# Conv-side output projection in a new block order, its neighbours' stores on other queues, norm weights spread by DMA

## The chip, the cores and the metric

One Trainium2 chip, one core, one execution of one program. The metric is device microseconds (us) from start to end of an execution. An execution is timed as a whole; the profile of one execution gives its span (first to last instruction) and every instruction in it. Engines in rows: PE is TensorE (PEld its weight loads), DVE is VectorE, ACT is ScalarE, POOL is GpSimd, SP is the engine that here does nothing but issue DMAs (SPq in rows).

## The reference, cut to what matters

```python
h = rms_norm(x, norm1_g)                       # x: 1024 tokens x 1024
u = h @ w_in                                   # conv gate 2x512, then q, k, v, g of 512 each
a_out = conv_group(u_conv, ...)                # GLU, 31 causal taps, layer norm, silu -> 512 wide
b_out = retention_group(q, k, v, g, ...)       # 4 heads, chunks of 64 -> 512 wide
x = x + concat([a_out, b_out]) @ w_out         # output projection
h = rms_norm(x, norm2_g)
x = x + square(relu(h @ w_ff1)) @ w_ff2        # 1024 -> 4096 -> 1024
return rms_norm(x, final_g)
```

All of it is float32.

## The kernel before, in words

A float32 matmul is made of three passes over operands that are split into a high and a low part of a reduced type (`mm3`, L138 to L140: high by high, high by low, low by high). ACT makes the high part by a copy, DVE the low part by a subtraction (`split_evac`, L189 and L190). A matmul that depends on a fresh operand therefore waits for DMA, ACT and DVE in that order; the third pass, or the second, is the one that waits for DVE.

The 1024 tokens are 8 blocks of 128 (`blk[0..7]`). The stages around the change, in time:

1. Input projections, convolution taps and retention. Here ACT, DVE and SP load and split the weights.
2. Output projection, retention half (`ret_side`, L515 to L579), block by block, weights `wo`.
3. The second norm's weights, a vector of 1024, are spread over all partitions as `n2row`: POOL makes eight 128x128 diagonals, PE multiplies each by ones, ACT copies the two banks (L605 to L611).
4. Output projection, conv half, the loop L669 to L681. In iteration b: layer norm of the conv output of block b+3 (`conv_norm`: PE transposes `py`, DVE statistics, POOL reciprocal root, ACT `yn`); its silu and split for block b+2 (`conv_side`: PE transposes `pt`, ACT `a` and `mh`, DVE `ml`); 24 matmuls of 128x512 for block b (`out_proj`); DVE adds them to `blk[b]` (L675); ACT takes the mean square (`trash`), POOL the root (`rn`); then `normed_columns(b - 1)`.
5. `normed_columns(b)` scales the block (DVE `xn`, L624), transposes it on PE (`pt`, L634), and makes columns for FF1, which runs one step of Strassen's scheme: seven products M1 to M7 of half-size operands. Blocks 0 to 3 are tokens of the first half: their columns are the operands B11 and B21 themselves (used by M1 and M2), are split, and are also stored whole to DRAM (`keep_columns`, DMA `colsB<-full`). Blocks 4 to 7 are of the second half. Block 4+t loads the columns of block t back (`b<-colsB`), and DVE forms from both T1, T2, B22, T3 and T4 (seven DVE instructions of 128x512, nine for block 7; called the T work below). T1, T2 and B22 are split in place. T3 and T4 of blocks 4 to 6 go to DRAM (`colsT<-b`), because their tiles come free only later, and return in one load of 768 KB each (`h<-colsT`, L829), after which ACT and DVE split them.
6. FF1, 16 pairs p of weight columns (`strassen_pair`). The first four pairs (AHEAD = 4) do M1 and M2 first, all four of them, since only B11 and B21 are needed; then pair 0 goes on with M6, M5, M7, M3, M4, and so do pairs 1 to 3. The other twelve do all seven products at once. A product is 12 matmuls of 128x512. Each pair's results, 7 tiles, are stored to DRAM (`x0M`, `x1M`, ...).
7. FF2 and the final norm.

Every DMA of the kernel before is issued by SP, in program order of its list: an SP instruction that waits for its data holds all behind it. Within each other engine too, instructions run in one order that a scheduler fixed when the kernel was built, by priorities that follow the order of the code. PSUM is two pools of four banks; `py`, `pt`, the `pb` of M2 and of odd products take one, `acc` and `pa` the other. So a transpose waits until a bank's former content has been read by ACT and DVE.

Of the kernel before, what the change touches and what calls it, by code (L numbers as in the profile page):

```python
# [8 lines left out]
F32 = mybir.dt.float32  # L9
F32R = mybir.dt.float32r  # L10
BF16 = mybir.dt.bfloat16
AF = mybir.ActivationFunctionType
ALU = mybir.AluOpType
PSUM = bass.MemoryType.PSUM

P = 128
D = 1024
# [8 lines left out]
ND = D // P  # L26
NB = S // P
NC = CW // P
NF = FF // P
HALF = 512  # L30
# [3 lines left out]
ALIGN = 256  # L34
QUOTA = (4, 16, 11, 11, 13, 33, 22, 14)
NPAIR = NF // 2
AHEAD = 4


@with_exitstack  # L40
def hybrid_layer_kernel(
# [14 lines left out]
    nc = tc.nc  # L56
# [6 lines left out]
    sp = pool("sp", 11)  # L63
    tiny = pool("tiny", 8)
# [4 lines left out]
    pr = pool("pr", 4, space=PSUM)  # L69
# [80 lines left out]
    def mean_sq(src):  # L150

        tr = sp.tile([P, D], BF16, tag="s", name="trash")
        ss = tiny.tile([P, 1], F32, tag="ss1", name="ss")
        nc.scalar.activation(tr, src, AF.Square, scale=D**-0.5, accum_out=ss)
        return ss
# [86 lines left out]
    def stats(t):  # L242

        nonlocal r1_pair
        xt = cp.tile([P, D], F32, tag="c", name="xt")
        nc.sync.dma_start(xt, x[t * P : (t + 1) * P, :])
        if t % 2 == 0 or t >= 4:
            r1_pair = const.tile([P, 2], F32, name=f"r1_{t}")
            r1[t] = r1_pair[:, 0:1]
        else:  # L250
            r1[t] = r1_pair[:, 1:2]
        m = tiny.tile([P, 1], F32, tag="nmr", name="m1")
        nc.gpsimd.tensor_tensor(m, mean_sq(xt), eps1, ALU.add)
        nc.gpsimd.tensor_tensor(r1[t], m, mhalf[:, 0:1], ALU.pow)
# [67 lines left out]
    nc.sync.dma_start(dec, decay)  # L322
    for t in range(NB):
        stats(t)

    first, accs = accs, [[bank(1)], [bank(1)]]
    for d in range(ND):
# [163 lines left out]
    def out_proj(wo, mh, ml):  # L491
        accs = []
        for n in range(2):
            acc = ps.tile([P, HALF], F32, tag="mm", name="acc")
            for c in range(NC):
                mm3(
                    acc, mh[:, c], ml[:, c],
                    wo[c][:, 0, 0, n * HALF : (n + 1) * HALF],
                    wo[c][:, 1, 0, n * HALF : (n + 1) * HALF],
                    c == 0, c == NC - 1,  # L500
                )
            accs.append(acc)
        return accs
# [34 lines left out]
    def conv_norm(b):  # L538

        py = pr.tile([P, NC, P], F32, tag="r", name="py")  # L540
        for c in range(NC):
            nc.tensor.transpose(out=py[:, c], in_=ys[c][:, b * P : (b + 1) * P], identity=ident)
        st = tiny.tile([P, 6], F32, tag="st", name="st")
        nc.vector.bn_stats(st, py.rearrange("p c e -> p (c e)"))
        mv = tiny.tile([P, 2], F32, tag="mv", name="mv")
        nc.vector.bn_aggr(mv, st)
        r = rstd_of(mv[:, 1:2], 1.0)
        yn = sp.tile([P, CW], F32, tag="s", name="yn")
        nmr = tiny.tile([P, 1], F32, tag="nmr", name="nmr")
        nc.gpsimd.tensor_scalar(nmr, mv[:, 0:1], r[:, 0:1], -1.0, ALU.mult, ALU.mult)  # L550
        nc.scalar.activation(
            yn, py.rearrange("p c e -> p (c e)"), AF.Identity, bias=nmr[:, 0:1], scale=r[:, 0:1]
        )
        normed[b] = yn

    def conv_side(b):

        yn = normed.pop(b)
        pt = pr.tile([P, NC, P], F32, tag="r", name="pt")
        for c in range(NC):  # L560
            nc.tensor.transpose(out=pt[:, c], in_=yn[:, c * P : (c + 1) * P], identity=ident)
        a = sp.tile([P, NC, P], F32, tag="s", name="a")
        for c in range(NC):
            nc.scalar.activation(a[:, c], pt[:, c], AF.Silu, bias=col("lb", c), scale=col("lg", c))
        sides[b] = split_tiles(a)

    marks.append(len(pe_log))
    for b in range(NB):
        if b + 2 < NB:
            rsides[b + 2] = ret_side(b + 2)  # L570
        if b == NB - 2:
            woa = load_wo(0, False)
        if b >= NB - 3:
            conv_norm(b - (NB - 3))
        if b >= NB - 2:
            conv_side(b - (NB - 2))
        (mh, ml), xr = rsides.pop(b)
        for n, acc in enumerate(out_proj(wo, mh, ml)):
            nc.vector.tensor_tensor(blk[b][:, n], acc, xr[n], ALU.add)  # L579
# [22 lines left out]
    dram_cols = {nm: xd.tile([P, 4, HALF], F32, name=f"cols{nm}") for nm in ("B11", "B21", "T3", "T4")}  # L602

    n2row = cp.tile([P, D], F32, tag="c", name="n2row")
    for g in range(2):  # L605
        pb = pr.tile([P, 4, P], F32, tag="r", name="pb")
        for i in range(4):
            diag = sp.tile([P, P], F32, tag="s", name="diag")
            nc.gpsimd.tensor_scalar(diag, ident, col("n2", 4 * g + i), None, ALU.mult)
            nc.tensor.matmul(pb[:, i], lhsT=ones, rhs=diag, start=True, stop=True)  # L610
        nc.scalar.activation(n2row[:, g * HALF : (g + 1) * HALF], pb.rearrange("p i t -> p (i t)"), AF.Copy)  # L611

    def new_columns(name, extra=False):
        hb[name] = [wp.tile([P, 4, HALF], F32R, tag="w", name="h2") for _ in range(1 if extra else 2)]
# [1 line left out]
            hb[name].append(hx.tile([P, 4, HALF], F32R, name="tx"))  # L616

    def keep_columns(name, cols, t):
        nc.sync.dma_start(dram_cols[name][:, :, cols], t)

    def normed_columns(b, r):

# [39 lines left out]
        for name, full in (("T3", b12), ("T4", b21)):  # L662
            if b < NB - 1:
                keep_columns(name, cols, full)
            else:
                split_evac(full, *hl(name))

    rn = {}
    for b in range(NB):  # L669
        if b + 3 < NB:  # L670
            conv_norm(b + 3)
        if b + 2 < NB:
            conv_side(b + 2)
        for n, acc in enumerate(out_proj(woa, *sides.pop(b))):
            nc.vector.tensor_tensor(blk[b][:, n], acc, blk[b][:, n], ALU.add)  # L675
        m = tiny.tile([P, 1], F32, tag="nmr", name="m2")
        nc.gpsimd.tensor_tensor(m, mean_sq(flat(b)), eps1, ALU.add)
        rn[b] = tiny.tile([P, 1], F32, tag="r1", name="rn")
        nc.gpsimd.tensor_tensor(rn[b], m, mhalf[:, 0:1], ALU.pow)
        if b >= 1:  # L680
            normed_columns(b - 1, rn.pop(b - 1))  # L681

# [29 lines left out]
    def split_named(ops, raw, names):  # L714
        hi, lo = split_pairs(raw)
        for k, nm in enumerate(names):
            ops[nm] = hi[:, k], lo[:, k]
# [12 lines left out]
    xs = {}  # L730

    def keep(p, name, t):
        nc.sync.dma_start(xs[p][name], t)

    def square(src, rl=None):

# [27 lines left out]
    def strassen_pair(p, ahead):  # L764

        a, b = {}, hb

        def product(acc, name, first, last):
            for d in range(4):
                mm3(  # L770
                    acc, a[name][0][:, d], a[name][1][:, d], b[name][0][:, d], b[name][1][:, d],
                    first and d == 0, last and d == 3, loose=True,
                )

        def copy(acc):
            t = sp.tile([P, HALF], F32, tag="s", name="part")
            nc.scalar.activation(t, acc, AF.Copy)
            return t

        def plus(acc, t):  # L780
            nc.vector.tensor_tensor(t, acc, t, ALU.add)
            return t

        raw = [load_w1(2 * p + i) for i in range(1 if ahead else 2)]
        split_named(a, raw[0], ("M1", "M2"))
        if not ahead:
            prep_sums(a, raw)
        pa = ps.tile([P, HALF], F32, tag="mm", name="pa")
        product(pa, "M1", True, False)
        m1 = copy(pa)  # L790
        pb = pr.tile([P, HALF], F32, tag="r", name="pb")
        product(pb, "M2", True, True)
        c11 = square(plus(pb, m1))
        if p < NPAIR - 1:
            keep(p, "M1", c11)
        if ahead:
            yield
            prep_sums(a, [load_w1(2 * p + i) for i in range(2)])
            c11 = sp.tile([P, HALF], F32, tag="s", name="hid")
            nc.sync.dma_start(c11, xs[p]["M1"])  # L800
        product(pa, "M6", False, False)
        u2 = copy(pa)
        pb = pr.tile([P, HALF], F32, tag="r", name="pb")
        product(pb, "M5", True, False)
        m5 = copy(pb)
        product(pa, "M7", False, False)
        c22 = square(plus(pa, m5))
        product(pb, "M3", False, True)
        c12 = square(plus(pb, u2))
        product(pa, "M4", False, True)  # L810
        c21 = square(pa, relu(pa))
        if p < NPAIR - 1:
            keep_operands(p, c11, c12, c21, c22)
        else:
            for i, row in enumerate(((c11, c12), (c21, c22))):
                for j, t in enumerate(row):
                    nc.sync.dma_start(last_hid[i][:, j * HALF : (j + 1) * HALF], t)

    last_hid = [xd.tile([P, S], F32, name=f"hid{i}") for i in range(2)]
    for p in range(NPAIR):  # L820
        new_operands(p)
    pairs = [strassen_pair(p, p < AHEAD) for p in range(NPAIR)]
    hb["M1"], hb["M2"] = hb["B11"], hb["B21"]
    next(pairs[0])
    for name in ("T3", "T4"):
# [2 lines left out]
    for name in ("T3", "T4"):  # L828
        nc.sync.dma_start(hb[name][1][:, :, early].bitcast(F32), dram_cols[name][:, :, early])  # L829
    normed_columns(NB - 1, rn.pop(NB - 1))  # L830
    for p in range(1, AHEAD):
        next(pairs[p])
    for name in ("T3", "T4"):
        hi, lo = (t[:, :, early] for t in hb[name])
# [201 lines left out]
```

## Time and profile before

| | us |
|---|---|
| median of 3 runs | 1069.08 (1068.64 to 1069.27) |
| profiled execution, its own time | 1070.16 |
| its span in the trace | 1068.4 |
| PE busy | 1036.5 (97%) |
| DVE busy | 805.9 (75%) |
| ACT busy | 378.9 (35%) |
| POOL busy | 69.7 (7%) |
| mean granted clock of PE | 0.987 |

Times in the rows count from the start of the span. The profiled execution lies 1.08 us above the median. PE is busy almost throughout; where it isn't, or where its granted clock falls, is what the rows below show, stage by stage.

### The profile page before, as it was taken

The numbers are of one execution on the slowest core, as the hardware profiler recorded it, in microseconds if no ns is written. First come the engines' busy times: TensorE is split into PE (matmuls) and PEld (weight loads), VectorE is DVE, ScalarE is ACT, GpSimd is POOL, SyncE is SP. The second block draws the span as 40 slices with busy tenths as digits, with TensorE's granted clock in tenths as the row PEclk, the third lists the DMA queues.
The fourth block names the chain that finished last, engine by engine and source line by source line (L and its number), as shares of the span: only waits on it lengthen the run. The fifth ranks groups of instructions, "written<-read, shape, count | busy, mean of one in ns | idle before, by whom it ended". The sixth has DMA issues, their size and how long they took to land.

```text
span 1068.4 us, 12644 instructions
## 1 busy us (share of the span) xinstructions
PE 1036.5 (97%) x4760; PEld 858.1 (80%) x4760; DVE 805.9 (75%) x998; ACT 378.9 (35%) x602; POOL 69.7 (7%) x134
## 2 busy tenths in 40 slices
PE   9999999999999997899999999999999999999996
PEld 7888888888888775677888888888788888888885
DVE  6397769998796367866777676776898778777857
ACT  7511111144521565432332333323443333433423
POOL 0400110022000311000000000000000000000003
PEclk9999999999999999889999999999999999999998
DMA  9412011002242013635545344356546355253324
GB/s 359 162 45 79 20 59 60 21 1 80 65 152 79 1 60 114 195 136 178 195 143 183 138 161 145 137 178 232 182 164 246 104 177 176 92 183 102 91 78 157
DMA packets 59676, 136.98 MB, mean 128 GB/s; under 512 B 5600, under 2 KB 18016, under 8 KB 59616
## 3 DMA queue, kind: packets, MB, share of 16 engines
q1 hardware_dynamic: 59616, 136.19, 37.0%
q8 instruction: 37, 0.61, 0.2%
q14 instruction: 23, 0.19, 0.1%
HBM read 99.73 MB, written 36.44 MB: 127 GB/s over the span
## 4 chain that ended last, share of the span: by engine, by line
PE 50%; DVE 3%; DMA 3%; issue 2%; ACT 1%; POOL 1%; SPq 0%; POOLq 0%; DVEq 0%; ACTq 0%
PE acc L138 9%; PE acc L140 9%; PE acc L139 9%; PE pa L140 5%; PE pa L139 5%; PE pa L138 5%; PE pb L140 3%; PE pb L139 3%; PE pb L138 3%; DMA raw<-in_w_dram 2%; DMA xr<-x1M 1%; DVE w1l L190 1%; DVE ot L933 0%; DVE hid L740 0%; DMA w2raw<-in_w_dram 0%
## 5 line engine op out<-in xcount | busy, mean ns | idle before, releaser
L138 PE MATMUL acc<-w 128*128 128x512 f32 x454 | 176.7, 389 | 1.1 <-ACT w L189 1.1
L139 PE MATMUL acc<-w 128*128 128x512 f32 x454 | 176.2, 388 | 0.0
L140 PE MATMUL acc<-w 128*128 128x512 f32 x454 | 175.9, 388 | 0.0
L380 DVE SCALAR_TENSOR_TENSOR y<-glu,vec,y 128x1024 f32<-128x1024 f32 x120 | 153.8, 1290 | 2.0
L138 PEld LDWEIGHTS acc<-w 128*128 128x128 f32 x454 | 85.2, 188 | 20.1 <-ACT w L189 1.5
L138 PE MATMUL acc<-w,cols 128*128 128x512 f32 x256 | 100.1, 391 | 0.0
L139 PE MATMUL acc<-w,cols 128*128 128x512 f32 x256 | 99.8, 390 | 0.0
L140 PE MATMUL acc<-w,cols 128*128 128x512 f32 x256 | 99.7, 390 | 0.0
L139 PEld LDWEIGHTS acc<-w 128*128 128x128 f32 x454 | 85.2, 188 | 17.5
L140 PEld LDWEIGHTS acc<-w 128*128 128x128 f32 x454 | 85.2, 188 | 17.5
L189 ACT ACTIVATE w<-xr 128x1024 fp32r<-128x1024 f32 (+1 forms) x56 | 56.2, 1004 | 107.4 <-PE acc L140 57.9
L140 PE MATMUL pa<-h,w1l 128*128 128x512 f32 x192 | 77.8, 405 | 11.6 <-DVE w1l L190 11.6
L190 DVE TENSOR_TENSOR w<-xr,w 128x1024 fp32r<-128x1024 f32 (+1 forms) x56 | 64.7, 1155 | 28.1 <-ACT w L189 27.9
L905 DVE TENSOR_TENSOR blk<-acc,blk 128x512 f32<-128x512 f32 x112 | 72.8, 686 | 11.7 <-PE acc L140 11.7
L138 PE MATMUL pa<-h,w1h 128*128 128x512 f32 x192 | 77.0, 402 | 0.1
L140 PE MATMUL pb<-h,w1l 128*128 128x512 f32 x192 | 75.5, 393 | 0.0
L138 PE MATMUL pb<-h,w1h 128*128 128x512 f32 x192 | 75.3, 392 | 0.0
L139 PE MATMUL pb<-h,w1h 128*128 128x512 f32 x192 | 75.2, 392 | 0.0
L115 ACT ACTIVATE w<-raw 128x1024 fp32r<-128x1024 f32 (+1 forms) x36 | 34.8, 967 | 96.2 <-PE acc L140 70.5
L189 ACT ACTIVATE w1h<-t 128x1024 fp32r<-128x1024 f32 x32 | 33.8, 1059 | 65.9 <-PE pb L140 40.5
L140 PEld LDWEIGHTS acc<-w,cols 128*128 128x128 f32 x256 | 48.1, 188 | 10.0
L138 PEld LDWEIGHTS acc<-w,cols 128*128 128x128 f32 x256 | 48.1, 188 | 9.8
(175 smaller groups left out, 1962.7 us busy)
## 6 DMA issues: line engine op xcount, KB each, us to landing
raw<-in_w_dram SPq DMA_DIRECT2D x38, 512.0 KB, 3.5
w2raw<-in_w_dram SPq DMA_DIRECT2D x30, 512.0 KB, 4.5
raw<-in_w_in_dram SPq DMA_DIRECT2D x23, 512.0 KB, 3.3
xt<-in_x_dram SPq DMA_DIRECT2D x8, 512.0 KB, 7.7
raw<-in_w_out_dram SPq DMA_DIRECT2D x8, 512.0 KB, 3.3
xr<-in_x_dram SPq DMA_DIRECT2D x16, 256.0 KB, 3.1
out_dram<-ot SPq DMA_DIRECT2D x16, 256.0 KB, 2.0
xcol<-in_x_cols_dram SPq DMA_DIRECT2D x7, 512.0 KB, 7.2
```

Of the source, the lines that this page charges most:

```text
L115: nc.scalar.activation(w[:, 0, i], raw[:, i], AF.Copy)
L138: nc.tensor.matmul(acc, lhsT=lh, rhs=rh, start=first, stop=False, **kw)
L139: nc.tensor.matmul(acc, lhsT=lh, rhs=rl, start=False, stop=False, **kw)
L140: pe_log.append(nc.tensor.matmul(acc, lhsT=ll, rhs=rh, start=False, stop=last, **kw))
L189: nc.scalar.activation(hi, src, AF.Copy)
L190: nc.vector.tensor_tensor(lo, src, hi.bitcast(F32), ALU.subtract)
L380: nc.vector.scalar_tensor_tensor(y, glu[c][:, k : k + S], tap(k), y, ALU.mult, ALU.add)
L905: nc.vector.tensor_tensor(t, acc[lane][r], t, ALU.add)
```

## The change

Four edits. (1) The loop of stage 4 visits the blocks in the order 0 1 4 2 5 3 6 7, and so do the layer norms and silus ahead of it. The loop's code now stands behind the creation of the pairs. (2) `colsB` is stored from ACT's queue, `colsT`, all results of FF1 and the last hidden tiles from POOL's; SP keeps the loads. (3) `n2row` is made without PE: eight columns of the small-vector tile are written to DRAM as 1024 numbers near the start, on SP behind the token loads, and read back spread over all partitions. (4) The first W1 tiles of pairs 0 and 1 are loaded and split inside the loop, at its last two iterations, and those of pairs 2 and 3 one step sooner than their products.

```diff
+ORDER = (0, 1, 4, 2, 5, 3, 6, 7)
...
     for t in range(NB):
         stats(t)
+    n2d = xd.tile([D], F32, name="n2d")
+    nc.sync.dma_start(n2d.rearrange("(d p) -> p d", p=P), vec[:, cols["n2"] : cols["n2"] + ND])
...
     n2row = cp.tile([P, D], F32, tag="c", name="n2row")
-    for g in range(2):
-        pb = pr.tile([P, 4, P], F32, tag="r", name="pb")
-        for i in range(4):
-            diag = sp.tile([P, P], F32, tag="s", name="diag")
-            nc.gpsimd.tensor_scalar(diag, ident, col("n2", 4 * g + i), None, ALU.mult)
-            nc.tensor.matmul(pb[:, i], lhsT=ones, rhs=diag, start=True, stop=True)
-        nc.scalar.activation(n2row[:, g * HALF : (g + 1) * HALF], pb.rearrange("p i t -> p (i t)"), AF.Copy)
+    nc.sync.dma_start(n2row, n2d.partition_broadcast(P))
...
     def keep_columns(name, cols, t):
-        nc.sync.dma_start(dram_cols[name][:, :, cols], t)
+        eng = nc.scalar if name in ("B11", "B21") else nc.gpsimd
+        eng.dma_start(dram_cols[name][:, :, cols], t)
...
     def keep(p, name, t):
-        nc.sync.dma_start(xs[p][name], t)
+        nc.gpsimd.dma_start(xs[p][name], t)
...
         split_named(a, raw[0], ("M1", "M2"))
+        if ahead:
+            yield
...
     pairs = [strassen_pair(p, p < AHEAD) for p in range(NPAIR)]
+    rn = {}
+    for i, b in enumerate(ORDER):
+        if i + 3 < NB:
+            conv_norm(ORDER[i + 3])
+        if i + 2 < NB:
+            conv_side(ORDER[i + 2])
...
+        if i >= 6:
+            next(pairs[i - 6])
+        if i >= 1:
+            normed_columns(ORDER[i - 1], rn.pop(ORDER[i - 1]))
```

What this does to the engines' orders, at three places. (Line numbers differ by one to twenty between the two kernels; the number behind a name tells tiles apart.)

DVE, where the T work of block 4 stands. Before, it begins behind block 5's `xn_3377` and goes on among the sums of block 6, the seventh in order (`pt_3312` are block 4's columns; `h2_2981` belongs to block 3):

```order
L190 TENSOR_TENSOR h2_2981<-pt_3241,h2_2980 128x4x128
L675 TENSOR_TENSOR blk5_106<-acc_3270,blk5_106 128x512
L190 TENSOR_TENSOR ml_3267<-a_3261,mh_3266 128x512
L675 TENSOR_TENSOR blk5_106<-acc_3283,blk5_106 128x512
L624 SCALAR_TENSOR_TENSOR xn_3377<-blk5_106,rn_3303,n2row_2805 128x1024
L655 TENSOR_TENSOR b11_3323<-b12_3327,b11_3323 128x512
L675 TENSOR_TENSOR blk6_107<-acc_3342,blk6_107 128x512
L656 TENSOR_TENSOR t2_3328<-pt_3312,b11_3323 128x512
L659 TENSOR_TENSOR b12_3327<-pt_3312,b12_3327 128x512
```

DVE now: the same T work (`pt_3186` are block 4's columns) stands between block 2's `xn_3282` and block 2's own columns (`pt_3284`, `pt_3289`).

```order
L622 SCALAR_TENSOR_TENSOR xn_3282<-blk2_103,rn_3177,n2row_2807 128x1024
L653 TENSOR_TENSOR b11_3197<-b12_3201,b11_3197 128x512
L815 TENSOR_TENSOR blk5_106<-acc_3247,blk5_106 128x512
L654 TENSOR_TENSOR t2_3202<-pt_3186,b11_3197 128x512
L657 TENSOR_TENSOR b12_3201<-pt_3186,b12_3201 128x512
L658 TENSOR_TENSOR b21_3198<-b21_3198,t2_3202 128x512
L191 TENSOR_TENSOR tx_3192<-t2_3202,h2_3191 128x4x128
L191 TENSOR_TENSOR h2_3194<-b11_3197,h2_3193 128x4x128
L815 TENSOR_TENSOR blk5_106<-acc_3260,blk5_106 128x512
L191 TENSOR_TENSOR h2_3196<-pt_3186,h2_3195 128x4x128
L191 TENSOR_TENSOR h2_3012<-pt_3284,h2_3011 128x4x128
```

It moved from among the seventh block's sums to among the fifth's (block 5), two blocks up, and stands ahead of the splits that free the banks of block 2's transposes.

DVE at the first M1. Before, its low weights `w1l_3535` stand behind the T work of blocks 4 and 5 and among that of block 6 (`b11_3455`):

```order
L190 TENSOR_TENSOR h2_3322<-pt_3384,h2_3321 128x4x128
L655 TENSOR_TENSOR b11_3455<-b12_3459,b11_3455 128x512
L190 TENSOR_TENSOR w1l_3535<-raw_3532,w1h_3534 128x1024
L656 TENSOR_TENSOR t2_3460<-pt_3450,b11_3455 128x512
L190 TENSOR_TENSOR h2_3320<-b11_3455,h2_3319 128x4x128
```

Now `w1l_3422` (pair 0) stands ahead of the last two blocks' sums, and `w1l_3485` (pair 1) ahead of the T work of blocks 6 and 7:

```order
L815 TENSOR_TENSOR blk3_104<-acc_3331,blk3_104 128x512
L191 TENSOR_TENSOR w1l_3422<-raw_3419,w1h_3421 128x1024
L191 TENSOR_TENSOR ml_3315<-a_3309,mh_3314 128x512
L815 TENSOR_TENSOR blk6_107<-acc_3384,blk6_107 128x512
...
L815 TENSOR_TENSOR blk7_108<-acc_3460,blk7_108 128x512
L191 TENSOR_TENSOR w1l_3485<-raw_3482,w1h_3484 128x1024
L622 SCALAR_TENSOR_TENSOR xn_3488<-blk6_107,rn_3417,n2row_2807 128x1024
L622 SCALAR_TENSOR_TENSOR xn_3557<-blk7_108,rn_3480,n2row_2807 128x1024
L653 TENSOR_TENSOR b11_3500<-b12_3504,b11_3500 128x512
```

PE's order there, before (the last of the projection, `acc_3421`, then block 6's transposes, then M1 of pair 0 in `pa_3538` begun with two matmuls, M2 in `pb_3553` with two):

```order
L140 MATMUL acc_3421<-w_2676,ml_3267 128x512
L634 MATMUL pt_3445<-ident_89,xn_3443 128x128 x4
L634 MATMUL pt_3450<-ident_89,xn_3443 128x128 x4
L138 MATMUL pa_3538<-h2_2978,w1h_3534 128x512
L139 MATMUL pa_3538<-h2_2979,w1h_3534 128x512
L138 MATMUL pb_3553<-h2_2980,w1h_3534 128x512
L139 MATMUL pb_3553<-h2_2981,w1h_3534 128x512
L140 MATMUL pa_3538<-h2_2978,w1l_3535 128x512
```

and now: M1 of pair 0 (12 matmuls in `pa_3519`) follows the projection at once, then half of pair 1's M1 (`pa_3590`), and only then block 6's transposes.

```order
L141 MATMUL acc_3460<-w_2678,ml_3315 128x512
L139 MATMUL pa_3519<-h2_3011,w1h_3421 128x512
...
L141 MATMUL pa_3590<-h2_3011,w1l_3485 128x512
L632 MATMUL pt_3490<-ident_89,xn_3488 128x128 x4
L632 MATMUL pt_3495<-ident_89,xn_3488 128x128 x4
L139 MATMUL pb_3534<-h2_3013,w1h_3421 128x512
```

SP's queue before, from block 6's store of T3 on:

```order
L619 DMA colsT3_2803<-b12_3459 512x1x128
L619 DMA colsT4_2804<-b21_3456 512x1x128
L829 DMA h2_3571<-colsT3_2803 128x4x384
L829 DMA h2_3573<-colsT4_2804 128x4x384
L733 DMA x0M1_3476<-hid_3567 128x512
L651 DMA b11_3588<-colsB11_2801 128x4x128
```

and now, loads only:

```order
L687 DMA raw_3660<-in_w1_dram 128x1024
L830 DMA h2_3552<-colsT3_2805 128x4x384
L830 DMA h2_3554<-colsT4_2806 128x4x384
L649 DMA b11_3569<-colsB11_2803 128x4x128
```

The return of T3 and T4 (`h2_3552`, `h2_3554`) still waits for block 6's stores, which POOL now issues.

## Rows read from the trace of the kernel before

**Rows 1.** Windows of 20 us: their length; PE, PEld, DVE, ACT, POOL busy; PEclk; DMA.
```profile
400.00:420.00 20.00, 17.78 (x86) 14.27 (x84) 12.35 (x18) 11.17 (x23) 2.18 (x6) 1.00 0.37 107
420.00:440.00 20.00, 14.82 (x59) 11.79 (x60) 17.69 (x23) 10.17 (x15) 0.77 (x3) 0.74 0.63 204
440.00:460.00 20.00, 15.76 (x58) 12.15 (x56) 14.57 (x22) 8.25 (x12) 0.00 (x0) 0.83 0.38 123
```

**Rows 2.** PE's waits over the whole run: us in total, times, longest.
```profile
PE pa L140 <- DVE w1l L190: 11.6, 5, 3.8
PE pt L634 <- DVE xn L624: 3.7, 2, 2.3
```

**Rows 3.** Timeline of PE between the halves: start, duration, instruction, [idle before].
```profile
357.47 0.61 PE L610 MATMUL pb<-diag,ones 128*128 128x128 f32 x4
...
361.65 0.60 PE L542 MATMUL py<-ident,y 128*128 128x128 f32 x4
...
362.44 0.48 PE L138 MATMUL acc<-w,mh 128*128 128x512 f32 x1
...
363.22 0.39 PE L138 MATMUL acc<-w,mh 128*128 128x512 f32 x1
363.44 0.39 PE L139 MATMUL acc<-w,mh 128*128 128x512 f32 x1
```

**Rows 4.** Timeline of PE, from block 4's columns to M6.
```profile
412.70 1.06 PE L634 MATMUL pt<-ident,xn 128*128 128x128 f32 x8 [1.46 <-DVE xn L624]
...
418.85 0.39 PE L140 MATMUL acc<-w,ml 128*128 128x512 f32 x1
421.50 1.15 PE L634 MATMUL pt<-ident,xn 128*128 128x128 f32 x8 [2.27 <-DVE xn L624]
...
428.04 0.79 PE L140 MATMUL pa<-h,w1l 128*128 128x512 f32 x1 [3.67 <-DVE w1l L190]
...
432.05 0.63 PE L140 MATMUL pa<-h,w1l 128*128 128x512 f32 x1
432.47 0.46 PE L140 MATMUL pb<-h,w1l 128*128 128x512 f32 x1
...
461.81 0.50 PE L140 MATMUL pa<-h,w1l 128*128 128x512 f32 x1 [2.27 <-DVE w1l L190]
```

**Rows 5.** Timeline of DVE: T work of block 4, then pieces towards M6.
```profile
412.48 0.69 DVE L655 TENSOR_TENSOR b<-b,b 128x512 f32<-128x512 f32 x1
413.08 0.68 DVE L675 TENSOR_TENSOR blk<-acc,blk 128x512 f32<-128x512 f32 x1
...
416.68 0.68 DVE L190 TENSOR_TENSOR h<-pt,h 128x512 fp32r<-128x512 f32 x1
...
432.70 1.22 DVE L190 TENSOR_TENSOR w1l<-raw,w1h 128x1024 fp32r<-128x1024 f32 x1
...
451.91 1.75 DVE L190 TENSOR_TENSOR h<-h,h 128x1536 fp32r<-128x1536 f32 x1
```

**Rows 6.** Timeline of ACT: the split of T3 waits for its load; block 6's copy.
```profile
424.23 0.58 ACT L654 ACTIVATE b<-pt 128x512 f32<-128x512 f32 x1
...
437.16 1.49 ACT L189 ACTIVATE h<-h 128x1536 fp32r<-128x1536 f32 x1 [2.90 <-DMA h<-colsT]
```

**Rows 7.** Timeline of SP's queue: block 6's stores, the loads.
```profile
429.82 1.71 SPq L619 DMA_DIRECT2D colsT<-b  x2
432.52 1.62 SPq L829 DMA_DIRECT2D h<-colsT  x2
```

**Rows 8.** DMA issues: KB each, median us from issue to landing.
```profile
x3M<-xsum SPq DMA_DIRECT2D x8, 256.0 KB, 3.0
...
colsT<-b SPq DMA_DIRECT2D x6, 256.0 KB, 2.5
h<-colsT SPq DMA_DIRECT2D x2, 768.0 KB, 5.4
```

**Rows 9.** A window near the start, columns as rows 1.
```profile
34.00:38.00 4.00, 4.00 (x20) 3.30 (x19) 0.00 (x0) 0.00 (x0) 3.50 (x7) 1.00 0.03 10
```

**Rows 10.** Timeline of ACT near the start: first split of the next weights.
```profile
40.97 1.05 ACT L115 ACTIVATE w<-raw 128x1024 fp32r<-128x1024 f32 x1
```

More of the change, by code (lines that the diff above doesn't have):

```diff
@@ L573, in hybrid_layer_kernel @@
         if b >= NB - 3:
-            conv_norm(b - (NB - 3))
+            conv_norm(ORDER[b - (NB - 3)])
         if b >= NB - 2:
-            conv_side(b - (NB - 2))
+            conv_side(ORDER[b - (NB - 2)])
         (mh, ml), xr = rsides.pop(b)
@@ L666, in normed_columns @@
                 split_evac(full, *hl(name))
[L668 to L681, printed above, removed]
     NAMES = ("M1", "M2", "M6", "M5", "M7", "M3", "M4")
@@ L816, in strassen_pair @@
                 for j, t in enumerate(row):
-                    nc.sync.dma_start(last_hid[i][:, j * HALF : (j + 1) * HALF], t)
+                    nc.gpsimd.dma_start(last_hid[i][:, j * HALF : (j + 1) * HALF], t)
     last_hid = [xd.tile([P, S], F32, name=f"hid{i}") for i in range(2)]
@@ L822, in hybrid_layer_kernel @@
     pairs = [strassen_pair(p, p < AHEAD) for p in range(NPAIR)]
+    rn = {}
[4 more added lines that the diff above has]
+            conv_side(ORDER[i + 2])
+        for n, acc in enumerate(out_proj(woa, *sides.pop(b))):
+            nc.vector.tensor_tensor(blk[b][:, n], acc, blk[b][:, n], ALU.add)
+        m = tiny.tile([P, 1], F32, tag="nmr", name="m2")
+        nc.gpsimd.tensor_tensor(m, mean_sq(flat(b)), eps1, ALU.add)
+        rn[b] = tiny.tile([P, 1], F32, tag="r1", name="rn")
+        nc.gpsimd.tensor_tensor(rn[b], m, mhalf[:, 0:1], ALU.pow)
+        if i >= 6:
+            next(pairs[i - 6])
+        if i >= 1:
+            normed_columns(ORDER[i - 1], rn.pop(ORDER[i - 1]))
     hb["M1"], hb["M2"] = hb["B11"], hb["B21"]
@@ L830, in hybrid_layer_kernel @@
     normed_columns(NB - 1, rn.pop(NB - 1))
-    for p in range(1, AHEAD):
+    next(pairs[1])
+    for p in range(2, AHEAD):
+        next(pairs[p])
         next(pairs[p])
```

## The prediction

> **What bounds the kernel now.** I read the windows of 20 us first, to find where PE is not full. It is full at full clock but for the stretch of the change: of 20 us it is busy 17.78 in 400 to 420, 14.82 in 420 to 440 and 15.76 in 440 to 460, with a granted clock of 0.74 and 0.83 in the last two [rows 1]. So PE sets the end, and what can be won is its idle and half-clock time there. The list of PE's waits names the releaser: 11.6 us for DVE's `w1l`, 3.7 us for DVE's `xn` [rows 2]. DVE is not short of work there, 17.69 of 20 us [rows 1]: it stands behind T work that arrives together with the first products' weights. The third view is PE's timeline between the halves: from 357.47 to 361.65, 4.18 us, PE does the eight diagonals alone, waiting for POOL between them; the first matmul of the conv half starts at 362.44 [rows 3]. The fourth is PE's timeline up to M6 (M6's first low-weight matmul stands in for M6): stalls of 1.46, 2.27, 3.67 us, and 2.27 before M6 at 461.81 [rows 4]. At full clock matmuls follow at 0.227 us [rows 3]; behind the stall of 3.67 us they follow at 0.42, half clock [rows 4].
>
> **The ceiling.** Diagonals 4.2, idle after them 11.6 + 3.7 + about 1 of small waits, and half clock: some 34 matmuls at 0.2 more each, 6.8, an estimate from the two paces. Together 27. Nothing else is touched that PE waits for, so no gain can pass 27 us (1043).
>
> **Norm weights by DMA.** PE loses 4.18 us of work that nothing hides, so block 0 starts at 358.3 instead of 362.4. The price is two DMAs on SP. The first, of 1024 single numbers, stands behind the token loads; DMA is nearly idle (share 0.03) from 34 to 38 [rows 9], and ACT comes to the next weights at 40.97 only [rows 10], so up to 6 us of delay are covered; beyond that each us costs a us. No row shows such a DMA; below, 0; above, I take a 256 KB store's 3.0 [rows 8]. Taken: 0. The second lands long before the conv half. Gain 4.2.
>
> **The conv half.** Before, block 0 to the last matmul at 418.85 [rows 4] took 56.6 us, of which 2.4 are stalls (1.46 at block 4's columns, 0.9 small): 54.2 clean. Now a stall appears. T work of block 4 stands among block 5's sums, ahead of the splits of block 2, and holds the bank of block 4's second transpose; DVE takes from the T work's first row at 412.48 to its last at 416.68 some 4.8 us [rows 5], and one of its rows waits for a projection sum. PE, which after block 5's matmuls wants that bank for block 2's columns, stalls between 2.0 us (if ACT's copies interleave well) and 3.8; I take 3.7, since ACT's silu stands between its copies. ACT also issues eight column stores inside the loop that paces the blocks; SP's two take 1.71 with a wait in them [rows 7], so 0 to 0.9 each, of which I take 1.5 us in all on the path. End: 358.3 + 54.2 + 3.7 + 1.5 = 417.7, against 419.1: the head start is mostly given back here.
>
> **M1 and M2.** They follow at once, since `w1l` of pair 0 is split before: stalls of 2.27 and 3.67 go, and a later one of the 11.6 [rows 2, 4]. 96 matmuls at 0.227 are 21.8, 16 transposes 2.0 (eight take 1.15 [rows 4] or less): all four pairs are done at 441.5, or 444 with one more wait of 2.5.
>
> **M6, the next late thing.** M6 needs `w1l` of pair 0's sums, which stand in DVE's order behind the split of T3 and T4, that is behind the return of those columns. Chain: 417.7 + 18 matmuls 4.1 = 421.8, block 6's transposes 0.8, ACT's copy 0.6 [rows 6], three DVE rows at 0.6 [rows 5] = 425.0. Then POOL's store of T3: no row shows a store from POOL. Below it is SP's, 0.5 to 0.6 (two DMAs of three quarters of a MB hold SP 1.62 [rows 7]), above it is 3.0, the time of a whole store to landing [rows 8]. I take 1.0, near SP's, since the sizes are the same. Landing 2.5, load 5.4 [rows 8]: 433.9. ACT's split 1.5 [rows 6]: 435.4. Then DVE from the split of T3 to the weights of M6 in its order: two splits at 1.7, eight rows of block 7's T work, eleven other rows of 128x512 at 0.6 and one `w1l` of 1.2 [rows 5]: 3.4 + 11.4 + 1.2 = 16.0. M6 at 451.4, 10.4 before 461.81 [rows 4]. PE then idles 8 to 9 us ahead of M6, a longer stall than any before, and some 12 matmuls behind it go at half clock (2.4, against 1.6 now): I take off 1.0 for that.
>
> **W1 splits, stores of FF1.** The splits cost the same rows, earlier. A pair of FF1 is 84 matmuls, 19.05 us at 0.227, and has seven stores, so POOL (busy 0.77 us or less per 20 [rows 1]) hides them as long as one takes under 2.7 us of POOL's time. Nothing waits for a finished store soon. Taken: 0.
>
> **Sum.** 1070.16 (the profiled run) - 10.4 + 1.0 = 1060.8; the median lies 1.1 below its profiled run, so 1059.7, rounded 1060. Changing POOL's 1.0 per store to its ends moves M6 by -0.5 or +4 (two stores on the way).
>
> **A rule that speaks against it.** DVE's rows of 512 columns follow at 0.60, those of 1024 take twice that [rows 5]: one pace for all, so no row here runs in a faster mode. The Trainium skill ("SBUF — State Buffer", SBUF: two separate sides) says that a DMA issued from GpSimd starves while DVE is in a two-port mode, since its descriptors are written over the port that DVE then locks: about 620 ns alone and 3100 ns overlapped. By that rule FF1's seven stores would take 21.7 us in a pair of 19.05, rival (c) below; the even pace of the rows says that DVE isn't in that mode, and no run here shows a store from GpSimd yet. The Trainium skill ("DMA: Bandwidth & Descriptors", Issuing engines are not separate DMA queues) says that several issuing engines save only the time of issue: by it the stores' move is worth nothing in itself.
>
> **Rivals.** (a) *POOL's column stores are slow.* 2.5 to 3 us each instead of 1, two on the way of T4 and, for block 4, two ahead of block 5's `rn` in POOL's order, which holds `xn`, so PE: 4 us at M6 and 1 to 3 at the projection. Gain 3 to 6: 1064 to 1067. For it: no price in the trace. Against it: the same bytes as SP's. (b) *The stalls shrink.* Block 4's T work finishes in time (3.7 back) and the clock stays up (1 to 2), or T3 returns sooner than the median 5.4: 1048 to 1055. For it: those loads ran in a window with DMA 0.63 busy [rows 1], which is quieter if traffic moves; against it: M6's 16 us of DVE rows stay. (c) *Slower: POOL can't keep up in FF1.* If a store holds POOL as long as it takes to land, 3.0 [rows 8], seven take 21, 1.95 more than a pair gives; DVE's results then have no free tiles. Over 13 of the pairs +25, less the 9 won: 1085. It decides at 2.7 us a store. For it: no row prices a store from POOL; against it: SP's 0.5 to 0.6 for the same bytes. (d) *No change.* The late T3 keeps M6 where it is: POOL's two stores and a stalled projection cost the 10 us again, 1068 to 1070; it needs 5 us per store or a second stall of 4.
>
> **Chances.** My forecast, 1055 to 1064: 0.54. (a) 0.18, (b) 0.14, (c) 0.08, (d) 0.06. Differences under 0.2% (2.1 us) can't be told from none here. Faster by more: 0.54 + 0.14 + most of (a) = 0.84; same: (d) and the edge of (a), 0.07; slower: (c) and an unlooked-for delay near the start, 0.09. The range 1051 to 1068 holds the forecast, (a), and over half of (b).
>
> **What would show it.** No `pb` between the halves, block 0 about 358; a stall of 2 to 4 us in the conv half before block 2's columns are transposed; M1 right behind the projection near 418; one long PE stall before M6, which starts near 451; POOL's stores under 2.7 us in FF1, no PE idle there beyond that of before. Wrong if POOL's rows are long, if ACT's issues stretch the loop by more than 1.5, if the clock falls in the projection (each us of half clock costs half a us), or if the first weights after 40.97 are late.

## The result and the profile after

The changed kernel takes 1063.11 us (median) against 1068.77 us of the kernel before, run beside it: a ratio of 0.9946, 95% interval 0.993 to 0.9962, so 4.1 to 7.5 us faster. One execution of five, at a mean granted clock of 0.848, is left out of the ratio. The profiled execution took 1062.97 us, its span is 1061.2: 7.2 less than the profiled one before.

The windows of the changed kernel that answer to [rows 1] and [rows 9] (length, busy time of PE, PEld, DVE, ACT, POOL, then PEclk, DMA share, GB/s):

```profile
34.00:38.00 4.00, 4.00 (x20) 3.30 (x19) 0.00 (x0) 0.00 (x0) 3.27 (x7) 1.00 1.08 79
...
400.00:420.00 20.00, 20.00 (x101) 16.57 (x100) 17.19 (x23) 12.96 (x24) 5.13 (x9) 1.00 0.61 184
420.00:440.00 20.00, 18.13 (x84) 14.56 (x82) 14.46 (x21) 9.84 (x15) 2.01 (x3) 1.00 0.59 197
440.00:460.00 20.00, 11.85 (x41) 9.40 (x42) 15.43 (x22) 7.11 (x10) 1.62 (x3) 0.66 0.39 131
```

PE's loss has not gone so much as gathered: 400 to 420 is full now, 440 to 460 is worse than before (11.85 against 15.76, clock 0.66 against 0.83). The list of PE's waits over the run, which answers to [rows 2] (total, times, longest):

```profile
PE pa L139 <- ACT w1h L190: 10.0, 1, 10.0
PE pa L139 <- ACT part L760: 2.3, 1, 2.3
PE pa L141 <- DVE w1l L191: 2.2, 2, 1.2
```

Five waits of 11.6 us in all for `w1l` and two of 3.7 for `xn` have become one of 10.0, ahead of M6, a new one of 2.3, and two for `w1l` of 2.2. Added up over PE's timeline from 300 to 1000 us, waits are 17.8 us before and 16.9 after: the change took away hardly any idle time. What it took away is the diagonals (4.2 us of busy PE) and half clock: PE was busy for 15.0 us at a granted clock of 0.50 in that stretch before and for 9.1 after, some 3.0 us less lost (an estimate: half of the difference). PE's timeline, which answers to [rows 3, 4]:

```profile
43.22 0.50 PE L139 MATMUL acc<-cols,w 128*128 128x512 f32 x1 [0.89 <-ACT row L342]
...
357.91 0.60 PE L545 MATMUL py<-ident,y 128*128 128x128 f32 x4
...
393.84 1.04 PE L632 MATMUL pt<-ident,xn 128*128 128x128 f32 x8
...
396.99 0.66 PE L564 MATMUL pt<-ident,yn 128*128 128x128 f32 x4 [0.50 <-ACT a L567]
...
414.03 0.39 PE L141 MATMUL acc<-w,ml 128*128 128x512 f32 x1
414.26 0.39 PE L139 MATMUL pa<-h,w1h 128*128 128x512 f32 x1
...
448.15 0.79 PE L139 MATMUL pa<-h,w1h 128*128 128x512 f32 x1 [10.02 <-ACT w1h L190]
...
449.60 0.63 PE L141 MATMUL pa<-h,w1l 128*128 128x512 f32 x1
...
476.50 0.50 PE L139 MATMUL pa<-h,a 128*128 128x512 f32 x1 [0.95 <-DVE part L764]
...
732.58 0.50 PE L139 MATMUL pa<-h,w1h 128*128 128x512 f32 x1 [2.32 <-ACT part L760]
```

The reader follows the lead over the kernel before as it grows and shrinks. Transposes of block 0: 357.91 against 361.65, 3.7 ahead. Last matmul of the projection: 414.03 against 418.85, 4.8. M1 follows at the next row, without a gap. M6's first low-weight matmul: 449.60 against 461.81, 12.2. By the middle of FF1 it is 10.1 (a store of pair 6's results is issued at 563.44 by POOL, and was at 573.53 by SP), and 7.2 at the end. Of the 2.1 us lost in FF1 only 0.4 go in half clock (the granted clock is 0.50 from M6's start to 453.82, but the kernel before had a stretch of it behind M6 too). Some 1.3 go in waits of pairs 1 to 3, 3.2 us in all against 1.8 before; the new one among them is the 0.95 at 476.50, for a sum of DVE's. Another 2.9 go at the passage from FF1 to FF2: the stall of 2.32 at 732.58 and 1.7 of half clock behind it, less the 1.10 that stood among FF2's first matmuls before.

What M6 waits for, first from POOL, SP, ACT and DVE in turn (timelines; answering to [rows 5 to 7]):

```profile
421.98 0.74 POOL L617 DMA_DIRECT2D colsT<-b  x1 [3.71 <-DVE b L657]
...
568.72 0.54 POOL L716 DMA_DIRECT2D x3M<-hid  x1 [4.73 <-DVE hid L723]
```

```profile
424.65 2.36 SPq L830 DMA_DIRECT2D h<-colsT  x2
427.13 0.56 SPq L649 DMA_DIRECT2D b<-colsB  x1
```

```profile
41.62 1.06 ACT L116 ACTIVATE w<-raw 128x1024 fp32r<-128x1024 f32 x1 [0.75 <-DMA raw<-in_w_in_dram]
...
429.31 1.49 ACT L190 ACTIVATE h<-h 128x1536 fp32r<-128x1536 f32 x1 [5.67 <-DMA h<-colsT]
...
447.04 2.26 ACT L190 ACTIVATE w1h<-t 128x1024 fp32r<-128x1024 f32 x2 [5.14 <-DVE t L680]
...
730.99 1.06 ACT L190 ACTIVATE w<-w2raw 128x1024 fp32r<-128x1024 f32 x1 [8.25 <-DMA w2raw<-in_w_dram]
731.95 0.58 ACT L760 ACTIVATE part<-pa 128x512 f32<-128x512 f32 x1
```

```profile
430.83 1.76 DVE L191 TENSOR_TENSOR h<-h,h 128x1536 fp32r<-128x1536 f32 x1 [3.23 <-ACT h L190]
434.69 0.69 DVE L653 TENSOR_TENSOR b<-b,b 128x512 f32<-128x512 f32 x1 [2.10 <-DMA b<-colsB]
...
442.26 1.75 DVE L191 TENSOR_TENSOR h<-h,h 128x1536 fp32r<-128x1536 f32 x1
...
448.13 1.22 DVE L191 TENSOR_TENSOR w1l<-t,w1h 128x1024 fp32r<-128x1024 f32 x1
```

DVE waits 3.23 us for ACT's half of T3's split, which waits for the columns' return; then 2.10 for block 7's `b<-colsB`, whose loads stand behind that return on SP; then it does block 7's T work, T4's split and only then pair 0's sums and M6's weights. A store of FF1 holds POOL for 0.54 us, a column store for 0.71 to 0.92. The DMA issues that answer to [rows 8], and one near the start:

```profile
x3M<-xsum POOLq DMA_DIRECT2D x8, 256.0 KB, 2.7
...
colsT<-b POOLq DMA_DIRECT2D x6, 256.0 KB, 2.6
h<-colsT SPq DMA_DIRECT2D x2, 768.0 KB, 6.0
...
trg<-in_trig_dram SPq DMA_DIRECT2D x1, 512.0 KB, 16.4
```

### The profile page after: what moved, and what is told of

It is laid out like the page before. It is cut to its first block, busy times and chain, and to the rows that moved or that the text cites. A ratio compares the mean times of both kernels' runs of the same rounds, so it can differ in the third digit from the quotient of the medians.

```text
span 1061.2 us, 12636 instructions
## 1 busy us (share of the span) xinstructions
PE 1030.1 (97%) x4744; PEld 854.5 (81%) x4744; DVE 804.8 (76%) x998; ACT 377.0 (36%) x600; POOL 129.4 (12%) x241
## 4 chain that ended last, share of the span: by engine, by line
PE 80%; DVE 8%; DMA 5%; issue 3%; ACT 2%; POOL 1%; SPq 1%; POOLq 0%; DVEq 0%; ACTq 0%
PE acc L139 18%; PE acc L140 18%; PE acc L141 18%; PE pa L139 5%; PE pa L141 5%; PE pa L140 5%; PE pb L139 3%; PE pb L140 3%; PE pb L141 3%; DVE y L383 2%; DMA raw<-in_w_in_dram 2%; DMA raw<-in_w_dram 1%; DMA w2raw<-in_w_dram 1%; DMA b<-colsB 1%; DVE hid L723 1%
```

## The experiments

Every ratio is to the kernel before, run beside the variant.

My theory after the result: the diagonals are worth their 4 us; block order, W1 move and stores only gather PE's waits in front of M6, whose own chain (the columns' return, T work of block 7, splits, sums) is in DVE's order; and the stores cost something at the start of FF2. Rivals: the stores' move off SP is the gain, or the block order is.

**The norm weights alone.** In the kernel before, only these lines:

```diff
+    n2d = xd.tile([D], F32, name="n2d")
+    nc.sync.dma_start(n2d.rearrange("(d p) -> p d", p=P), vec[:, cols["n2"] : cols["n2"] + ND])
...
+    nc.sync.dma_start(n2row, n2d.partition_broadcast(P))
```

> The kernel before with the norm weights spread by DMA, nothing else. My theory: PE loses the 4.2 us of diagonals, which nothing hid, and everything behind moves up with it; the element-wise store near the start costs 0.6 of that. About 1065.2 us (ratio 0.9966), and the stalls in 390 to 510 are the same ones, 4 us earlier. Rival: what PE waits for from 390 on (DVE's T work, the returned columns) doesn't move up, the first stalls grow by what was saved: 1068 to 1069, no difference.

Measured: 1065.34 us against 1068.81, ratio 0.997 (0.9958 to 0.9982), as my theory said. PE's timeline of this run:

```profile
423.76 0.80 PE L140 MATMUL pa<-h,w1l 128*128 128x512 f32 x1 [4.54 <-DVE w1l L190]
...
447.32 0.80 PE L140 MATMUL pa<-h,w1l 128*128 128x512 f32 x1 [4.12 <-DVE w1l L190]
```

Both stalls stand 4 us earlier than in [rows 4] and in the run before, and are not much larger (4.54 against 3.67, 4.12 against 3.79). So 3.5 us of the 5.7 come from here. The element-wise store took its time, though: 4 KB, 15.4 us from issue to landing.

```profile
n2d<-vec SPq DMA_DIRECT2D x1, 4.0 KB, 15.4
```

**The stores alone.** In the kernel before:

```diff
-        nc.sync.dma_start(dram_cols[name][:, :, cols], t)
+        eng = nc.scalar if name in ("B11", "B21") else nc.gpsimd
+        eng.dma_start(dram_cols[name][:, :, cols], t)
...
-        nc.sync.dma_start(xs[p][name], t)
+        nc.gpsimd.dma_start(xs[p][name], t)
```

> The kernel before with only the stores moved to ACT's and POOL's queues. My theory: nobody waits for them on SP, so nothing is won around M6; but with FF1's stores gone from SP the order that was fixed for ACT puts the first split of FF2's weights ahead of a copy that FF1's last pair needs, which costs a stall of 2.3 us and 1.7 us of half clock less the 1.1 us stall that it replaces: 2.9. About 1071.7 us. Rival: SP's queue held the loads back, and the stores' move is what brought the gain: 1062 to 1066.

Measured: 1072.7 us, ratio 1.0042 (1.0028 to 1.0057): slower, as expected, so the rival falls. But not quite as I had it:

```profile
457.81 0.79 PE L138 MATMUL pa<-h,w1h 128*128 128x512 f32 x1 [10.91 <-ACT w1h L189]
...
754.79 0.50 PE L138 MATMUL acc<-w 128*128 128x512 f32 x1 [2.20 <-DVE hid L741]
```

The start of FF2 costs a stall of 2.20 where there was one of 1.10, behind FF2's first eleven matmuls and not in the last pair. Of the 2.7 us by which the span grew that is the smaller part: M6's first low-weight matmul is even 2.6 us earlier than before (459.25), but by pair 6 the run is 1.4 us behind (a store at 574.97 against 573.53): half clock behind the long stall and behind a later wait, and waits of pairs 1 to 3, 3.6 us against 1.8. That one long stall ahead of M6 is here already, in natural block order and with W1 unmoved.

**All stores back on SP, in the changed kernel.** The reverse of the diff above.

> The changed kernel with all its stores issued by SP again. My theory: the stall at the start of FF2 goes (2.9 us back), M6 stays within 2 us of where it is: 1060 to 1063 us. Rival: the columns' return waits behind stores on SP, M6 is late by 4 us or more, 1064 to 1068.

Measured: 1063.01 us, ratio 0.9948 (0.9936 to 0.996), the same as the changed kernel. The stall at the start of FF2 is gone (0.58 in its place), but this run's profile has others:

```profile
44.91 0.54 PE L139 MATMUL acc<-cols,w 128*128 128x512 f32 x1 [2.55 <-ACT row L342]
...
400.73 1.11 PE L564 MATMUL pt<-ident,yn 128*128 128x128 f32 x4 [2.26 <-ACT a L567]
...
455.13 0.80 PE L139 MATMUL pa<-h,w1h 128*128 128x512 f32 x1 [9.49 <-ACT w1h L190]
```

M6 begins at 455.13, 7.0 us later than in the changed kernel, where I had allowed 2: the stall near 45, which comes with the element-wise store (2.55 here, 0.89 there), the one in the projection, and half clock behind each. The pairs behind M6 and the start of FF2 give it back. So the stores' move trades a stall of 2.26 us in the projection for one at the start of FF2, and comes out at nothing.

**The order at the start of FF2, by hand.** In the changed kernel, ACT's first split of FF2's weights is tied behind the last copy of FF1:

```diff
+        hi = nc.scalar.activation(w[:, 0], src, AF.Copy)
+        if copies:
+            dep = copies.pop()
...
+            tc.add_manual_dep(
+                hi.ins if hasattr(hi, "ins") else hi,
+                (dep.ins if hasattr(dep, "ins") else dep).name,
...
```

> The changed kernel with one order fixed by hand: ACT's first split of FF2's weights stands behind the copies of FF1's last pair. My theory: the stall of 2.3 us before the last pair's M7 and the half clock behind it go, and a stall of about 1 us comes back at FF2's first matmul: 1060.2 us (ratio to the kernel before 0.992). Rival: FF2's first weights are then late by as much, and PE waits the 2.3 us there: 1062 to 1063.

Measured: 1061.72 us, ratio 0.9941 (0.9929 to 0.9953). The wait for `part` is gone, but:

```profile
741.96 0.50 PE L139 MATMUL acc<-w 128*128 128x512 f32 x1 [1.91 <-DVE hid L723]
```

A stall of 1.91 us stands behind FF2's first nine matmuls, where PE waits for DVE. DVE comes to that tile behind a split of FF2's weights, for whose load (`w2raw`) ACT waits 6.31 us in this profile. The rival was nearer: most of the stall moved. The 1.4 us between the medians lies inside both intervals.

**The split late.** The step that my theory blames. In the changed kernel, pair 0's sums come ahead of the split of T3 and T4, and the loads of T3 and T4 go behind block 7's (the edit does both):

```diff
             nc.sync.dma_start(c11, xs[p]["M1"])
+            yield
         product(pa, "M6", False, False)
...
+    normed_columns(NB - 1, rn.pop(NB - 1))
     for name in ("T3", "T4"):
         nc.sync.dma_start(hb[name][1][:, :, early].bitcast(F32), dram_cols[name][:, :, early])
-    normed_columns(NB - 1, rn.pop(NB - 1))
...
+    next(pairs[0])
     for name in ("T3", "T4"):
         hi, lo = (t[:, :, early] for t in hb[name])
         split_evac(lo.bitcast(F32), hi, lo)
```

> The changed kernel with the split of the returned T3 and T4 columns behind pair 0's sums in the code (a yield more), and their loads behind block 7's. Nothing is computed otherwise. My theory: M6's stall of 10.0 us is the DVE order, sums standing behind the split that waits for the columns' return; now M6's low weights come at about 441, 2 to 3 us of stall stay, the half clock behind it shrinks: 1052 to 1057 us. Rival: M6 is held by block 7's T work or by the loads of pair 0's weights, or the stall only moves to M7, which needs T3: 1060 us or more.

Measured: 1054.49 us, ratio 0.9876 (0.986 to 0.9892): 8.6 us less than the changed kernel. PE's timeline, then DVE's, then SP's:

```profile
438.82 0.50 PE L139 MATMUL pa<-h,w1h 128*128 128x512 f32 x1 [0.23 <-ACT w1h L190]
...
441.77 0.50 PE L141 MATMUL pa<-h,w1l 128*128 128x512 f32 x1 [1.76 <-DVE w1l L191]
```

```profile
427.99 0.69 DVE L653 TENSOR_TENSOR b<-b,b 128x512 f32<-128x512 f32 x1
...
440.50 1.22 DVE L191 TENSOR_TENSOR w1l<-t,w1h 128x1024 fp32r<-128x1024 f32 x1
...
442.24 1.22 DVE L191 TENSOR_TENSOR w1l<-t,w1h 128x1024 fp32r<-128x1024 f32 x1
443.37 1.75 DVE L191 TENSOR_TENSOR h<-h,h 128x1536 fp32r<-128x1536 f32 x1
```

```profile
417.39 0.52 SPq L649 DMA_DIRECT2D b<-colsB  x1
```

M6's weights stand ahead of the split now, the stall of 10.0 us is one of 0.23 and one of 1.76, and M7 doesn't wait. DVE does block 7's T work from 427.99 without a wait, since its loads go out at 417.39 instead of 427.13. So much of the cause of M6's stall is shown: its weights stood behind the columns' return, in DVE's order and, by way of block 7's loads, in SP's; it was not the amount of DVE's work, which is the same. How much each of the two orders counts is not shown. By the changed kernel's rows, an estimate: the loads turned alone would save about the 2.10 us for which DVE waits for block 7's, the split alone about T4's 1.75, since block 7's columns would land as late as before. Pair 0's first low weights come 7.6 us sooner here (440.50 against 448.13), so by this estimate it took both.

**The natural block order.** In the changed kernel, `ORDER = (0, 1, 2, 3, 4, 5, 6, 7)`.

> The changed kernel with the blocks in their natural order, all else kept. My theory: the order moves T work of blocks 4 and 5 ahead of M1's weights, but M6's stall takes the gain up, so that it is worth little: 1063 to 1065 us. Rival: the order is what brings the part beyond the diagonals: 1066 to 1069.

Measured: 1063.52 us, ratio 0.9961 (0.9948 to 0.9973), within the noise of the changed kernel. M6's stall is 2.2 us longer instead:

```profile
450.83 0.80 PE L139 MATMUL pa<-h,w1h 128*128 128x512 f32 x1 [12.20 <-ACT w1h L190]
```

**W1's splits where they were.** In the changed kernel, without the new yield and the calls in the loop.

> The changed kernel with the W1 splits where they were before. My theory: the stalls before M1's low weights come back (2 to 6 us) and M6's stall shrinks by about as much, since its own chain doesn't move; what is lost is half clock, 1 to 2 us: 1063 to 1066 us. Rival: M1 and M2 are late and M6 too: 1067 us or more.

Measured: 1062.89 us, ratio 0.995 (0.9936 to 0.9964): no difference either. A stall of 1.42 comes back ahead of M1, less than the 2 to 6 that I expected, and M6's is 1.05 shorter:

```profile
415.83 1.06 PE L632 MATMUL pt<-ident,xn 128*128 128x128 f32 x8 [1.42 <-DVE xn L622]
...
448.61 0.80 PE L139 MATMUL pa<-h,w1h 128*128 128x512 f32 x1 [8.97 <-ACT w1h L190]
```

**All three mends together.** Late split, tied order at FF2, and the element-wise store moved on SP behind the fifteenth load of input weights.

> The split late as in the first of this call, the hand-fixed order at the start of FF2, and the element-wise store of the norm weights moved on SP from behind the token loads to between the loads of the last input weights. My theory: the first gives 1054, the second 1 us, the third 0.6 (nothing up to 4, by execution): 1051 to 1054 us. Rival: the gains don't add, since PE waits for DVE there anyway: 1055 to 1058.

Measured: 1051.84 us, ratio 0.9849 (0.9836 to 0.9863), 11.3 us less than the changed kernel. The same kernel once more (its name speaks of SP, its stores are on ACT and POOL all the same):

> The fastest kernel so far once more, unchanged, for a second profile: 1051 to 1053 us by either theory; it shows whether the stall near 43 us stays away with the later element-wise store.

One run of 1048.09 us, below the 1051 to 1053 expected. Near 43 us PE waits 0.25 and 0.26 us in these two profiles, as before the change (0.25). Where they differ is a stall among FF2's first matmuls, first profile and second:

```profile
732.18 0.50 PE L141 MATMUL acc<-w 128*128 128x512 f32 x1 [2.05 <-DVE hid L732]
```

```profile
729.94 0.50 PE L141 MATMUL acc<-w 128*128 128x512 f32 x1 [0.38 <-DVE hid L732]
```

ACT waits 6.33 us for a load of FF2's weights in the first and 4.78 in the second, and only the first has half clock behind the stall (3.41 us at 0.50). With one and the same order, the stall at the start of FF2 goes in these two profiles by how soon that load lands.

**The late split without the rest.** Only the norm weights by DMA and the late split, in the kernel before.

> The kernel before with the norm weights by DMA and the late split, but the old block order, stores on SP and the W1 splits where they were. Question: is the order worth something once M6 no longer stalls? My theory: yes. The stalls ahead of M1 and M2 (1.4, 2.2 and 4.5 us in the first run) stay, only those of pair 3's weights (4.1) and of M6 (1.6) go, with some half clock: 1057 to 1060 us, 3 us or more above the run with the late split in the changed kernel. Rival: order and W1 move are worth nothing here either: 1052 to 1055.

Measured: 1059.34 us, ratio 0.991 (0.9894 to 0.9926). 4.9 us above the late split in the changed kernel (3.9 when each is taken against the kernel before beside it), since the stalls ahead of M1 and its low weights are all there (1.47, and the two shown):

```profile
418.24 1.25 PE L630 MATMUL pt<-ident,xn 128*128 128x128 f32 x8 [2.26 <-DVE xn L620]
424.77 0.80 PE L140 MATMUL pa<-h,w1l 128*128 128x512 f32 x1 [3.58 <-DVE w1l L190]
```

So block order, W1 move and stores together are worth 4 to 5 us once M6 doesn't stall, and were worth 2 with M6's stall in place.

**The fastest with its stores on SP.**

> The fastest kernel so far with all stores on SP. My theory: the stores' queue is worth nothing at M6 even now, since they are off the path: 1051 to 1053 us. Rival: SP's loads for M6 (pair 0's weights, the returned columns) now wait behind stores that wait for DVE, M6 or M7 stalls by 2 us or more: 1054 to 1057.

Measured: 1051.93 us, ratio 0.984 (0.9821 to 0.9858), against 1051.84 and 0.9849 with the stores on ACT and POOL: no difference is shown. The single run of 1048.09 leaves room for one of up to 4 us. The stall in the projection is there again, the one at FF2 is not:

```profile
397.14 0.66 PE L564 MATMUL pt<-ident,yn 128*128 128x128 f32 x4 [2.26 <-ACT a L567]
...
739.14 0.50 PE L141 MATMUL acc<-w 128*128 128x512 f32 x1 [0.29 <-ACT w L873]
```

**The element-wise store late, alone**, in the changed kernel.

> The changed kernel with the element-wise store of the norm weights moved on SP from behind the token loads to between later weight loads, nothing else. My theory: ACT no longer waits for the first weights (0.75 and 2.42 us in two profiles), PE's stall near 43 goes back from 0.9 to 0.25, and up to 2.5 in some executions: 1061 to 1062.5 us, and a narrower spread. Rival: M6's stall takes it up, since it isn't set by when the projection begins: 1063 us.

Measured: 1061.91 us, ratio 0.9937 (0.9921 to 0.9952). `trg` lands 8.6 us after its issue instead of 16.4, and PE's early stall is 0.26; but 1.2 us between the medians lie inside the intervals, and the spread (1060.07 to 1064.86) is no narrower. That the stall goes is shown, that the time falls is not.

## Why the prediction was right

The time, 1060 forecast and 1063.11 measured, lies in the range, and faster was right; of the 9.4 us that the sum gave, 5.7 came by the medians and 7.2 between the two profiled executions. Part of that is luck: M6 came 1.8 us earlier than the sum had it, and 4.0 us that the sum didn't have were lost behind it. Step by step:

- **Norm weights, 4.2 us:** right in mechanism and size; alone 3.5 us (1.9 to 4.5). The price was wrong. I bounded the element-wise store by 3.0 us, since a store of 256 KB lands in that; it took 16.5 in the changed kernel and 14.1 to 16.0 in others, for 4 KB. The DMA share of 34 to 38 is 1.08 where it was 0.03, `trg` lands in 16.4 us instead of 8.3, and the 6 us of cover that I had counted were used up: ACT waits 0.75 us more, PE 0.6.
- **The conv half, 417.7:** wrong. It ended at 414.3. The stall of 3.7 us at block 2's columns did not come: they are transposed at 393.84 without a wait, while DVE is still at block 4's T work, so that work did not hold the bank that they wanted. 0.50 for ACT's silu stands near it, and the ACT issues cost nothing that shows. I had not followed which of the four banks the transposes would want.
- **M1 and M2, 441.5:** the mechanism is right; they ran without a wait and were done at 438.0, by the 3.4 us that the projection was early.
- **M6, 451.4:** right in mechanism, and 1.8 off (449.6). The stall was forecast as 8 to 9 us and was 10.0. The chain that I added up, the return, T3's split, DVE's rows, is what the late split showed to be the cause. Two errors in it cancel in part: ACT's split of T3 begins at 429.31 and not at 433.9, 4.6 earlier, and from its end to M6's first low-weight matmul it takes 18.8 us and not 16.0, of which 2.10 are the wait for block 7's loads, which the sum had at nothing. That M6 begins at 448.15 with, at 448.61 without the W1 move, fits the chain.
- **Half clock behind it, 1.0:** the right size: 5.7 us at half clock from M6's start, 3.4 before, so 1.1 more lost, 0.4 of it behind the matmul that stands for M6. But the lead falls by 2.1 us to the middle of FF1, since the waits of pairs 1 to 3 grew by 1.3, which the sum had at nothing.
- **Stores of FF1, taken as 0:** the step that failed most. POOL hides them with ease, 0.54 us each against the 2.7 at which it would decide, so rival (c) falls. But with the stores off SP, the orders of ACT and DVE around FF2's first weights came out differently: in the changed kernel ACT's split waits 8.25 us for `w2raw` with a copy behind it that the last pair needs. The lead falls by 2.9 us there. I had compared the orders only up to M6. Rival (a), slow column stores, falls too (0.71 to 0.92 us), (d) with it; (b) was right about the projection and wrong about M6.
- **Signs of being wrong:** two that I had named came, both small: the first weights behind 40.97 were late by 0.65, and PE was idle in FF1 where it had not been.

Of the Trainium skill's two rules, the one in "SBUF — State Buffer" (SBUF: two separate sides), that a DMA issued from GpSimd starves while DVE is in a two-port mode, did not show: stores issue in 0.54 us with DVE 14 to 17 of 20 us busy. That is no test of the rule, since no row tells DVE's mode; the even pace on which the prediction rested would look the same if all rows were in one mode. The one in "DMA: Bandwidth & Descriptors" (Issuing engines are not separate DMA queues), that other queues save only issue time, agrees with both pairs of runs: 1063.11 and 1063.01, 1051.84 and 1051.93 (where they differ, 1072.7 against 1068.81 in the kernel before, it is by stalls that other orders brought).

What stays open: how much of M6's stall each of the two orders made, DVE's and SP's; what FF2's start would cost if its first weights landed sooner (tying ACT's order moved most of the stall to FF2's first matmuls); and how much of the 1.2 us of the early store is real.

## What to carry to other kernels

When a stage's waits are moved earlier and the time hardly changes, look for the wait in which they have gathered: here 17.8 us of waits became 16.9, one of them 10 us long, and the edit that dissolved that one (what an engine and a load queue do first) was worth some 8 us, while block order, W1 move and stores, worth 4 to 5 us with it, were worth 2 without. Compare the engines' orders to the end of the program, not only at the edit: moving stores to another queue changed the orders at the start of FF2. A DMA of single numbers is not priced by its bytes: 4 KB took longer here than 256 KB in long rows.

## What the runs showed of the hardware

A store of 1024 separate 4-byte numbers (4 KB) from 128 partitions took 14.1 to 16.5 us from issue to landing beside full queues, and 9.3 to 9.9 where it was issued behind the fifteenth load of input weights; the 256 KB stores of [rows 8] took 2.5 to 3.0. It held other transfers up: at a DMA share of 1.08, 79 GB/s were moved, where the kernel before moved 422 at 1.03:

```profile
26.00:30.00 4.00, 4.00 (x19) 3.32 (x18) 0.00 (x0) 3.75 (x8) 2.46 (x10) 1.00 1.03 422
```

A store issued by POOL occupied POOL for 0.54 us (128 rows) to 0.71 to 0.92 us (512 rows). It landed 2.3 to 4.2 us after issue (medians by tile), 9.5 for the last pair's sums, which go out beside FF2's first loads; from SP the medians were 2.0 to 3.0. After 10.0 us of idle PE the twelve matmuls of M6 and one more ran at half clock, 5.7 us at a granted clock of 0.50. Stalls of 1.9 to 2.3 us at the start of FF2 had 3.41 us of half clock behind them in some profiles (2.32 in the changed kernel, 1.91 with the order tied) and none in another (2.20 with the stores alone).
